# A two-layer hybrid encoder on one core: one head's products with the values a tick later, some priorities moved, and the last output tiles stored in another order

## The chip, the core and the metric

The kernel runs on one core of a Trainium2 chip. Five engines work side by side, each through its own list of instructions in order: TensorE (PE in the profile, with its weight loads as PEld), VectorE (DVE), ScalarE (ACT), GpSimd (POOL) and SyncE (SP), which issues most of the DMAs. An engine waits on a semaphore where it needs another's result. The metric is the device time of one execution, in microseconds (us).

## The reference

Two layers on 512 tokens of width 1024, in float32, then a last norm. Cut to what matters:

```python
for i in range(DEPTH):                                   # 2 layers
    proj = rmsnorm(x, norm_mix[i]) @ w_in[i]
    qa, ka, va, glu_in, qc, kc, vc, gates = split(proj)
    ya = diff_attention(qa, ka, va, ...)                 # 4 heads
    yb = conformer_conv(glu_in, ...)                     # 31 taps, layernorm, silu
    yc = neighbourhood_attention(qc, kc, vc, rpb[i])     # 8 heads, 8 x 16 windows
    ga, gb, gc = split(sigmoid(gates))
    x = x + (ga*(ya @ w_br_a[i]) + gb*(yb @ w_br_b[i]) + gc*(yc @ w_br_c[i])) @ w_o[i]
    h = rmsnorm(x, norm_ffn[i])
    x = x + (silu(h @ w_ffn_gate[i]) * (h @ w_ffn_up[i])) @ w_ffn_down[i]
    x = x + sigmoid(rmsnorm(x, norm_ple[i]) @ w_ple_gate[i]) * (p[i] @ w_ple_in[i])
return rmsnorm(x, norm_final)

def diff_attention(...):   # per head: two score maps of 64 columns each, rotated q and k
    a = softmax(s[:, 0]) - lam * softmax(s[:, 1])
    o = a @ v
    return rmsnorm(o, subln_g) * (1.0 - lam_init)
```

## The kernel before, in words

**Data.** Activations lie transposed: blocks of 128 channels x 512 tokens. Every product runs as three matmuls on a high and a low part (`mm3`, lines 177 to 179): high x high, high x low, low x high. So each operand is split first: ScalarE copies the high part (`act`, line 143), VectorE subtracts it to get the low part (`tt`, line 157). Weights come 128x1024 at a time through three rotating buffers each for the raw, high and low form (names ending in `wr`, `wh`, `wl`), and their loads and splits are issued with a priority far ahead of their use.

**Names.** The first part of a name is the stage: `glu`, `natten` (neighbourhood attention), `diff` (differential attention), `gatea`/`gateb`/`gatec`, `conv`, `mergea`, `wo`, `ffn`, `ple` (the gated input embedding), `pin` (its products). The second part is the buffer: `mm` (3 PSUM buffers), `sc` (2), `tr` (2, for transposes) and `av` (1) are PSUM; `qk`, `x`, `rp`, `e`, `a`, `pt`, `v`, `y`, `t`, `sm`, `rc`, `z` are SBUF.

**What sets the order.** TensorE executes in the order in which the program is written. The other engines' lists are ordered by a scheduler, from priorities that follow the order of writing, unless a `high_priority(offset=...)` moves some ahead. Attention and norms are written as generators (`later`, `run`): after every 4 products of three matmuls (`chunk`), that is 12 matmuls, the program makes one `tick`, and generators whose time has come issue their next piece between the products of the stage that runs then. `yield 2` means: go on two ticks later. The 31 taps of the convolution (`conv_z`, line 160, VectorE) are given out a few at a time behind other VectorE or ScalarE work (`background(after, n)`), and those left over run at the start of `conv`.

**Differential attention.** `diff_in(head)` computes q and k, rotates them (`diff_rp`: four small DMAs per tile exchange 32-row groups, then products with the tables `diff_r` and a sum) and queues four `diff_unit`s, one for each 128 queries. A unit makes two score maps (`diff_sc`, line 808), their maxima (`diff_s`, line 905), the exponentials (`diff_a`, `diff_e`) and their weighted difference; every second unit transposes its half of the weights (`diff_tr`, line 862), splits them (`diff_pt`) and multiplies them with the values (`diff_av`, from `diff_pt` and `diff_v`). After the second half follows the head's norm (`norm`): the squares `diff_ss` are transposed (line 213), summed (`diff_sm`, line 215), scaled, raised to a power on GpSimd (`diff_rc`, line 222), and spread over all rows by four more transposes (line 226). `diff_v` splits the values for all heads, the last tile of tokens last.

**The end.** The last two blocks of `ple` and the last norm run on tiles of 128 tokens (`final`): for each tile `finish` computes the gate and the norm's column, and `store` scales the row's three parts and writes them: the low half (512 columns, ScalarE and its DMA queue), the middle and high quarters (VectorE, written from SP).

Of the kernel before, what the change touches and what calls it, by code (L numbers as in the profile page):

```python
# [14 lines left out]
AF = mybir.ActivationFunctionType  # L15
ALU = mybir.AluOpType
# [4 lines left out]
P = 128  # L21
# [4 lines left out]
D = 1024  # L26
KD = 8
# [15 lines left out]
EPS = 1e-6  # L43
# [18 lines left out]
class Net:  # L62
# [143 lines left out]
    def norm(self, sq, n, waits, done, spread=True, eps=None):  # L206


        nc = self.nc
        yield waits[0]  # L210
        st = self.ps("tr", (P, 4, P))
        for c in range(4):
            nc.tensor.transpose(st[:, c, :], sq[:, c * P:(c + 1) * P], self.ident)
        sm = self.sb("sm", [P, 4])
        nc.vector.tensor_reduce(out=sm, in_=st, op=ALU.add, axis=AX.X)
        ms = self.sb("sm", [P, 4])
        if eps is None:
            nc.vector.tensor_scalar(ms, sm, 1.0 / n, EPS, ALU.mult, ALU.add)
        else:
            self.stt(ms, sm, 1.0 / n, eps, ALU.mult, ALU.add)  # L220
        col = self.sb("rc", [P, 4])
        nc.gpsimd.tensor_tensor(col, ms, self.power, ALU.pow)
        yield waits[1]
        bc = self.ps("tr", (P, 4, P))
        for c in range(4):
            nc.tensor.transpose(bc[:, c, :], col[:, c:c + 1].to_broadcast([P, P]), self.ident)
        bc = bc.rearrange("p a b -> p (a b)")
        done(col, self.spread(bc) if spread else bc)
# [394 lines left out]
    def natten_in(self, pr, st, ys):  # L623

        self.phase = "natten"
        st4 = self.sb("qk", [P, 4, 512], F32R)
        k2 = self.sb("x", [P, 2, 512], F32R)
        nats = self.parts_of("kh", [512], 2, F32R)
        for s, off in enumerate((OFF_QC, OFF_KC)):
            ps = self.proj(off + pr * P)  # L630
            f = 1.0 if s else 0.125
            nat, low = nats[s], self.sb("t", [P, 512], F32R)
            if pr == 0:

                t = low.bitcast(F32)
                self.stt(t, ps, f, self.rb, ALU.mult, ALU.mult)
                ps, f = t, 1.0
            self.act(nat, ps, AF.Copy, scale=f)
            self.low = self.stt(low, ps, f, nat.bitcast(F32), ALU.mult, ALU.subtract)
            self.background(self.low, 4 if self.i else 5 * (pr > 0))  # L640
            self.stack(nat, low, st4[:, 2 * s:2 * s + 2], k2 if s else None)
        box = {}
        ys.append(self.sb("y", [P, 2, 512], F32R))
        for n in range(4):
            self.later(self.natten_unit(pr, n // 2, n % 2, st4, k2, st, box, ys[pr]),
                       4 if pr else 6, 2)
# [200 lines left out]
    def diff_unit(self, head, qt, st4, k2, st, box, ys):  # L847

        nc, i = self.nc, self.i
        half, t = qt // 2, qt % 2  # L850
        box[qt] = self.probs(st4, k2, qt, box["s0"])
        if t == 0:
            return
        yield 3
        ats = [box[2 * half], box[2 * half + 1]]
        pps = []
        for kp in range(2):
            pt = self.ps("tr", (P, 2, 256))
            for u in range(2):
                for t in range(2):  # L860
                    kc = 2 * kp + u
                    nc.tensor.transpose(pt[:, u, t * P:(t + 1) * P],
                                        ats[t][:, kc * P:(kc + 1) * P], self.ident)
            pp = self.sb("pt", [P, 2, 2, 256], F32R)
            self.split(pp[:, 0], pp[:, 1], pt)
            pps.append(pp)
        yield 2
        if half == 0:
            box["av"] = self.ps("av")
        av = box["av"]  # L870
        cs = slice((head % 2) * P, (head % 2) * P + P)
        for kp in range(2):
            for u in range(2):
                v = st["v"][2 * kp + u][:, head // 2].rearrange("p (a b) -> p a b", a=2)
                self.mm3(av[:, half * 256:half * 256 + 256], v[:, 0, cs], v[:, 1, cs],
                         pps[kp][:, 0, u], pps[kp][:, 1, u], kp * 2 + u == 0, kp * 2 + u == 3)
        if half == 0:
            return

        eps = self.sb("sm", [P, 4])  # L880
        self.stt(eps, box["s0"], EPS, box["s0"], ALU.mult, ALU.mult)
        o = self.sb("t", [P, 512])
        sq = self.sb("ss", [P, 512])
        self.act(sq, av, AF.Square)
        self.act(o, av, AF.Copy, scale=self.subg[:, i:i + 1])

        def done(col, bc):
            self.tt(o, o, bc, ALU.mult)
            y = self.sb("y", [P, 2, 512], F32R)
            self.split(y[:, 0, :], y[:, 1, :], o)  # L890
            ys.append(y)

        yield from self.norm(sq, P, (1, 2), done, spread=False, eps=eps)
# [363 lines left out]
    def ple(self, h, x, xs, pairs):  # L1257
        self.phase = "ple"
        nc, i = self.nc, self.i
        last = i == L - 1  # L1260
        hn, st = [], []
        for m in range(KD - 2 * last):
            g = self.sb("t", [P, 512])
            if m < KD - 2 * last:
                pi = self.embedded(m)
            if m != 1:
                pg = self.ps("mm")
            if m == 0:
                nxt = self.ps("mm")
                self.pair((pg, nxt), (self.a["w_pg"][i, 0], self.a["w_pg"][i, 1]), h)  # L1270
            elif m == 1:
                pg = nxt
            else:
                self.gemm(pg, self.a["w_pg"][i, m], h)

            def gate(pg=pg, g=g):
                self.tt(g, pg, self.rb, ALU.mult)
                self.act(g, g, AF.Sigmoid, table="sigmoid")

            self.ready(gate)  # L1280
            if last and m == 3:
                self.gains()
            def rest(m=m, pi=pi, g=g):
                self.tt(g, g, pi, ALU.mult)
                self.tt(x[m], x[m], g, ALU.add)
                if last:
                    hn.append(self.sb("h", [P, 512]))
                    self.act(hn[m], x[m], AF.Copy, scale=self.par(0, "fin", m))
                    self.sumsq(m, x[m], st)
                else:  # L1290
                    nc.sync.dma_start(xs[m], x[m])
                    hn.append(self.norm_chunk(m, x[m], self.par(i + 1, "mix", m), FIRST[1][m], st))

            self.ready(rest)
        if last:
            return self.final(h, x[KD - 2:], pairs, hn, st[0])
        self.i = i + 1
        self.main_norm(st[0], (3, 2), x=x)
        return hn
# [10 lines left out]
    def final(self, h, x, pairs, hn, most):  # L1310
# [3 lines left out]
        nc, i, mm = self.nc, self.i, self.nc.tensor.matmul  # L1314
# [14 lines left out]
        rbs = self.col  # L1329
# [16 lines left out]

        def finish(t):
            g = self.sb("t", [P, 256])
            self.act(g, pgs[t], AF.Sigmoid, table="sigmoid", scale=rbs[:, t:t + 1])
            self.tt(g, g, pis[t], ALU.mult)  # L1350
            v = self.sb("a", [P, 256])
            self.tt(v, g, pair[t][:, 256:], ALU.add)
# [3 lines left out]
                out=q, in0=v, in1=v, scale=1.0, scalar=0.0, op0=ALU.mult, op1=ALU.add,  # L1356
                accum_out=s)
            ms = self.sb("sm", [P, 1])
            self.stt(ms, s, 1.0 / D, part[:, t:t + 1], ALU.mult, ALU.add)
            col = self.sb("rc", [P, 1])  # L1360
            nc.gpsimd.tensor_tensor(col, ms, self.power[:, 0:1], ALU.pow)
            vs.append(v)
            columns.append(col)

        def store(t):
            col, two = columns[t], pair[t]
            r, out = rows[t], self.a["out"][t * P:(t + 1) * P]
            self.act(r[:, 0:512], low[t], AF.Copy, scale=col)
            nc.scalar.dma_start(out[:, 0:512], r[:, 0:512])
            self.stt(r[:, 768:], vs[t], col, self.gain, ALU.mult, ALU.mult)  # L1370
            if t == 3:
                nc.sync.dma_start(out[:, 768:], r[:, 768:])
            nc.vector.tensor_scalar(r[:, 512:768], two[:, 0:256], col, None, ALU.mult)
            end = 768 if t == 3 else D
            nc.sync.dma_start(out[:, 512:end], r[:, 512:end])

        pair, low, pgs, vs, columns = [], [], [], [], []
        places = ("av", "mm", "av", "sc")
        def inputs(t):
            pis.append(self.ps("sc", (P, 256)))  # L1380
# [6 lines left out]
        for t in range(4):  # L1387
# [4 lines left out]
            products(pg, wg, h, t, range(4))  # L1392
            if t == 1:
                chunks(0)
            if t in (1, 2):
                low.append(turn(places[t - 1], hn[0:4], t - 1))
            products(pg, wg, h, t, range(4, 8 if t == 3 else 6))
            if t == 1:
                sums = self.ps("mm", (P, 4))
# [15 lines left out]
                finish(0)  # L1415
            if t:
                finish(t)
            if t in (1, 2):
                store(t - 1)
        for t in (2, 3):  # L1420
            low.append(turn(places[t], hn[0:4], t))
            store(t)
        return None


# [112 lines left out]
```

## Time and profile before

| | |
|---|---|
| time, median of 3 runs | 1781.59 us (1780.82 to 1783.68) |
| the profiled execution's own time | 1781.65 us |
| its span in the trace | 1779.9 us |
| TensorE busy | 1767.4 us, 99% of the span |
| VectorE busy | 1372.7 us, 77% |
| ScalarE busy | 897.9 us, 50% |
| GpSimd busy | 63.5 us, 4% |
| instructions | 26531 |
| granted TensorE clock, mean | 1.00 of full speed |
| DMA, mean over the span | 145 GB/s, 257.51 MB |

The page gives busy time by engine, then the chain of work that ended last, followed back from the last instruction. A row of a timeline is: start, duration, engine, line, operation, result and sources (without buffer numbers), how many in a row, and in brackets how long the engine was idle before it and what ended that. Matmuls overlap in the pipe, so the time that one costs is the step from its start to the next start.

### The profile page before, as it was taken

Reading aid. Unit: us, or ns where it says so; the run is one execution under the profiler, and the core shown is the slowest. Engines: PE = TensorE matmul, PEld = TensorE weight load, DVE = VectorE, ACT = ScalarE, POOL = GpSimd, SP = SyncE. Lnnn points to the kernel's source line nnn. Section 1 sums busy time; section 2 is a strip of 40 time slices with the busy share of each in tenths; the row PEclk is TensorE's granted clock in tenths of the full one; section 3 lists DMA queues with packets and bytes.
Section 4 is the critical chain, followed back from the end, with each engine's and each line's share of the span. In section 5 each row is a group of like instructions: output and inputs, shape, how many; then the busy total and the mean of one; then the engine's idle time right before and its main releaser. Section 6 shows DMA issues by size and latency. Waiting matters only on the chain.

```text
span 1779.9 us, 26531 instructions
## 1 busy us (share of the span) xinstructions
PE 1767.4 (99%) x10019; PEld 1551.4 (87%) x10019; DVE 1372.7 (77%) x2113; ACT 897.9 (50%) x1480; POOL 63.5 (4%) x102
## 2 busy tenths in 40 slices
PE   9999999999999999999999999999999999999998
PEld 7888888888899899898878888888888998998987
DVE  7789787897877577577786788879878775775776
ACT  5566555425665255255545664563356652542544
POOL 0000000000010000000000000000000100100000
PEclk9999999999999999999999999999999999999999
DMA  5767443325556366253437564433363662663332
GB/s 190 190 180 189 125 130 93 104 97 163 198 157 180 131 166 189 79 141 115 159 121 189 177 181 119 133 87 107 101 199 133 196 190 84 186 181 107 116 110 95
DMA packets 98384, 257.51 MB, mean 145 GB/s; under 512 B 12880, under 2 KB 17616, under 8 KB 98256
## 3 DMA queue, kind: packets, MB, share of 16 engines
q1 hardware_dynamic: 90912, 231.00, 41.4%
q0 software_dynamic: 6336, 23.07, 7.1%
q8 instruction: 79, 1.29, 0.3%
q10 hardware_dynamic: 1008, 1.75, 0.3%
q14 instruction: 49, 0.40, 0.1%
HBM read 216.44 MB, written 7.86 MB: 126 GB/s over the span
## 4 chain that ended last, share of the span: by engine, by line
PE 96%; DVE 2%; issue 1%; DMA 0%; ACT 0%; SPq 0%; POOL 0%; POOLq 0%; DVEq 0%; ACTq 0%
PE ffn_sc L1100 14%; PE ffn_av L1100 7%; PE ffn_mm L177 4%; PE ffn_mm L178 4%; PE ffn_mm L179 4%; PE ffn_tr L1100 4%; PE mergea_mm L179 2%; PE mergea_mm L177 2%; PE mergea_mm L178 2%; PE wo_mm L178 2%; PE wo_mm L179 2%; PE wo_mm L177 2%; PE gateb_mm L178 2%; PE gateb_mm L179 2%; PE gateb_mm L177 2%; PE natten_mm L177 1%
## 5 line engine op out<-in xcount | busy, mean ns | idle before, releaser
L143 ACT ACTIVATE ffn_wh<-ffn_wr 128x1024 fp32r<-128x1024 f32 (+1 forms) x114 | 117.3, 1029 | 183.2 <-PE ffn_mm L178 102.7
L160 DVE SCALAR_TENSOR_TENSOR conv_z<-glu_z,pre_par,conv_z 128x512 f32<-128x512 f32 x240 | 179.3, 747 | 3.0
L157 DVE TENSOR_TENSOR ffn_wl<-ffn_wr,ffn_wh 128x1024 fp32r<-128x1024 f32 (+1 forms) x114 | 135.0, 1184 | 46.5 <-ACT ffn_wh L143 46.0
L1100 PE MATMUL ffn_sc<-wo_h,ffn_wh 128*128 128x256 f32 x704 | 130.4, 283 | 0.0
L1100 PEld LDWEIGHTS ffn_sc<-wo_h,ffn_wh 128*128 128x128 f32 x704 | 110.4, 192 | 0.8
L1100 PE MATMUL ffn_sc<-wo_h,ffn_wl 128*128 128x256 f32 x352 | 99.6, 283 | 0.0
L177 PE MATMUL ffn_mm<-ffn_z,ffn_wh 128*128 128x512 f32 x240 | 93.4, 389 | 0.0
L178 PE MATMUL ffn_mm<-ffn_z,ffn_wh 128*128 128x512 f32 x240 | 93.4, 389 | 0.0
L179 PE MATMUL ffn_mm<-ffn_z,ffn_wl 128*128 128x512 f32 x240 | 93.4, 389 | 0.0
L157 DVE TENSOR_TENSOR ffn_t<-ffn_mm,wo_r 128x512 f32<-128x512 f32 x48 | 33.1, 689 | 72.3 <-PE ffn_mm L179 72.3
L157 DVE TENSOR_TENSOR ffn_wl<-ffn_rp,ffn_wh 128x1024 fp32r<-128x1024 f32 x44 | 53.8, 1222 | 30.1 <-ACT ffn_wh L143 30.1
L143 ACT ACTIVATE mergea_wh<-mergea_wr 128x1024 fp32r<-128x1024 f32 (+1 forms) x32 | 27.1, 847 | 88.8 <-PE mergea_mm L178 80.4
L1100 PEld LDWEIGHTS ffn_sc<-wo_h,ffn_wl 128*128 128x128 f32 x352 | 67.5, 192 | 0.0
L1100 PE MATMUL ffn_sc<-wo_qk,ffn_wh 128*128 128x256 f32 x352 | 67.1, 283 | 0.0
L1100 PE MATMUL ffn_sc<-wo_v,ffn_wh 128*128 128x256 f32 x352 | 67.1, 283 | 0.0
L1100 PE MATMUL ffn_av<-wo_h,ffn_wh 128*128 128x256 f32 x352 | 65.3, 283 | 0.0
L143 ACT ACTIVATE ffn_wh<-ffn_rp 128x1024 fp32r<-128x1024 f32 x44 | 46.4, 1055 | 29.4 <-PE ffn_mm L178 17.5
L905 DVE TENSOR_REDUCE diff_s<-diff_sc 128x1 f32<-128x512 f32 x64 | 42.7, 685 | 16.1 <-PE diff_sc L808 15.9
L1100 PEld LDWEIGHTS ffn_sc<-wo_qk,ffn_wh 128*128 128x128 f32 x352 | 54.9, 192 | 0.0
L1100 PEld LDWEIGHTS ffn_av<-wo_h,ffn_wh 128*128 128x128 f32 x352 | 54.9, 192 | 0.0
L1100 PEld LDWEIGHTS ffn_sc<-wo_v,ffn_wh 128*128 128x128 f32 x352 | 54.9, 192 | 0.0
L179 PEld LDWEIGHTS ffn_mm<-ffn_z,ffn_wl 128*128 128x128 f32 x240 | 45.1, 188 | 9.4
(726 smaller groups left out, 5635.4 us busy)
## 6 DMA issues: line engine op xcount, KB each, us to landing
ffn_wr<-w_gu SPq DMA_DIRECT2D x66, 512.0 KB, 4.2
ffn_e<-w_gu SPq DMA_DIRECT2D x32, 512.0 KB, 3.4
ffn_e<-w_gu POOLq DMA_DIRECT2D x32, 512.0 KB, 8.0
ffn_wr<-w_fd SPq DMA_DIRECT2D x32, 512.0 KB, 4.7
natten_wr<-w_in SPq DMA_DIRECT2D x16, 512.0 KB, 4.5
natten_b<-bias SPq DMA_DIRECT2D x32, 256.0 KB, 4.3
gatec_wr<-w_in SPq DMA_DIRECT2D x16, 512.0 KB, 4.4
diff_wr<-w_in SPq DMA_DIRECT2D x16, 512.0 KB, 4.7
```

The source lines that it names most:

```text
L143: i = self.nc.scalar.activation(out, in_, func, **kw)
L157: return self.nc.vector.tensor_tensor(out, a, b, op)
L160: return self.nc.vector.scalar_tensor_tensor(out, a, s, b, op0, op1)
L177: mm(out, wh, ah, start=first, stop=False)
L178: mm(out, wh, al, start=False, stop=False)
L179: mm(out, wl, ah, start=False, stop=last)
L905: nc.vector.tensor_reduce(out=m[:, u:u + 1], in_=sc, op=ALU.max, axis=AX.X, negate=True)
L1100: mm(bank[:, u], w[:, u, kp], t, start=begin and n == 0, stop=False, skip_group_check=True)
```

## The change

There are five edits:

- **A.** In `diff_unit`, head 0's first half waits 3 ticks in place of 2 ahead of its products with the values. The 12 matmuls `diff_av` change places with 12 matmuls `diff_mm`, in both layers.
- **B.** For the last block of `ple` in the first layer, the gate and what follows it are issued with a priority 14 ahead.
- **C.** In `norm`, the scaling of the row sums is issued with a priority 30 ahead.
- **D.** In the second layer, the first two of the four `natten_in` calls give out 3 taps instead of 4 behind each of their two splits; the four taps taken away are left to `conv`.
- **E.** At the end, tile 1's transposes move from the middle of tile 2's products to behind all products, and its low half is written then. Tile 2's middle quarter is scaled on ScalarE in place of VectorE, and tile 2's scalings are held behind tile 3's gate and norm column.

```diff
         sm = self.sb("sm", [P, 4])
         nc.vector.tensor_reduce(out=sm, in_=st, op=ALU.add, axis=AX.X)
         ms = self.sb("sm", [P, 4])
-        if eps is None:
-            nc.vector.tensor_scalar(ms, sm, 1.0 / n, EPS, ALU.mult, ALU.add)
-        else:
-            self.stt(ms, sm, 1.0 / n, eps, ALU.mult, ALU.add)
+        with self.tc.high_priority(offset=30):
+            if eps is None:
+                nc.vector.tensor_scalar(ms, sm, 1.0 / n, EPS, ALU.mult, ALU.add)
+            else:
+                self.stt(ms, sm, 1.0 / n, eps, ALU.mult, ALU.add)
         col = self.sb("rc", [P, 4])
         nc.gpsimd.tensor_tensor(col, ms, self.power, ALU.pow)
         yield waits[1]
...
                 ps, f = t, 1.0
             self.act(nat, ps, AF.Copy, scale=f)
             self.low = self.stt(low, ps, f, nat.bitcast(F32), ALU.mult, ALU.subtract)
-            self.background(self.low, 4 if self.i else 5 * (pr > 0))
+            self.background(self.low, 3 + (pr > 1) if self.i else 5 * (pr > 0))
             self.stack(nat, low, st4[:, 2 * s:2 * s + 2], k2 if s else None)
         box = {}
         ys.append(self.sb("y", [P, 2, 512], F32R))
...
             pp = self.sb("pt", [P, 2, 2, 256], F32R)
             self.split(pp[:, 0], pp[:, 1], pt)
             pps.append(pp)
-        yield 2
+        yield 2 + (head == half == 0)
         if half == 0:
             box["av"] = self.ps("av")
         av = box["av"]
...
                 self.tt(g, pg, self.rb, ALU.mult)
                 self.act(g, g, AF.Sigmoid, table="sigmoid")
 
-            self.ready(gate)
+            ahead = 14 * (m == KD - 1)
+            with self.tc.high_priority(offset=ahead):
+                self.ready(gate)
             if last and m == 3:
                 self.gains()
             def rest(m=m, pi=pi, g=g):
...
                     nc.sync.dma_start(xs[m], x[m])
                     hn.append(self.norm_chunk(m, x[m], self.par(i + 1, "mix", m), FIRST[1][m], st))
 
-            self.ready(rest)
+            with self.tc.high_priority(offset=ahead):
+                self.ready(rest)
         if last:
             return self.final(h, x[KD - 2:], pairs, hn, st[0])
         self.i = i + 1
...
 
         def finish(t):
             g = self.sb("t", [P, 256])
-            self.act(g, pgs[t], AF.Sigmoid, table="sigmoid", scale=rbs[:, t:t + 1])
+            gated = self.act(g, pgs[t], AF.Sigmoid, table="sigmoid", scale=rbs[:, t:t + 1])
             self.tt(g, g, pis[t], ALU.mult)
             v = self.sb("a", [P, 256])
             self.tt(v, g, pair[t][:, 256:], ALU.add)
...
                 out=q, in0=v, in1=v, scale=1.0, scalar=0.0, op0=ALU.mult, op1=ALU.add,
                 accum_out=s)
             ms = self.sb("sm", [P, 1])
-            self.stt(ms, s, 1.0 / D, part[:, t:t + 1], ALU.mult, ALU.add)
+            ends.append((gated, self.stt(ms, s, 1.0 / D, part[:, t:t + 1], ALU.mult, ALU.add)))
             col = self.sb("rc", [P, 1])
             nc.gpsimd.tensor_tensor(col, ms, self.power[:, 0:1], ALU.pow)
             vs.append(v)
             columns.append(col)
 
-        def store(t):
+        def store_low(t):
+            r, out = rows[t], self.a["out"][t * P:(t + 1) * P]
+            self.act(r[:, 0:512], low[t], AF.Copy, scale=columns[t])
+            nc.scalar.dma_start(out[:, 0:512], r[:, 0:512])
+
+        def store_high(t):
             col, two = columns[t], pair[t]
             r, out = rows[t], self.a["out"][t * P:(t + 1) * P]
-            self.act(r[:, 0:512], low[t], AF.Copy, scale=col)
-            nc.scalar.dma_start(out[:, 0:512], r[:, 0:512])
-            self.stt(r[:, 768:], vs[t], col, self.gain, ALU.mult, ALU.mult)
+            high = self.stt(r[:, 768:], vs[t], col, self.gain, ALU.mult, ALU.mult)
             if t == 3:
                 nc.sync.dma_start(out[:, 768:], r[:, 768:])
-            nc.vector.tensor_scalar(r[:, 512:768], two[:, 0:256], col, None, ALU.mult)
+            if t == 2:
+                self.behind(self.act(r[:, 512:768], two[:, 0:256], AF.Copy, scale=col), ends[3][0])
+                self.behind(high, ends[3][1])
+            else:
+                nc.vector.tensor_scalar(r[:, 512:768], two[:, 0:256], col, None, ALU.mult)
             end = 768 if t == 3 else D
             nc.sync.dma_start(out[:, 512:end], r[:, 512:end])
 
-        pair, low, pgs, vs, columns = [], [], [], [], []
+        pair, low, pgs, vs, columns, ends = [], [], [], [], [], []
         places = ("av", "mm", "av", "sc")
         def inputs(t):
             pis.append(self.ps("sc", (P, 256)))
...
             products(pg, wg, h, t, range(4))
             if t == 1:
                 chunks(0)
-            if t in (1, 2):
-                low.append(turn(places[t - 1], hn[0:4], t - 1))
+            if t == 1:
+                low.append(turn(places[0], hn[0:4], 0))
             products(pg, wg, h, t, range(4, 8 if t == 3 else 6))
             if t == 1:
                 sums = self.ps("mm", (P, 4))
...
                 finish(0)
             if t:
                 finish(t)
+            if t == 1:
+                store_low(0)
             if t in (1, 2):
-                store(t - 1)
-        for t in (2, 3):
+                store_high(t - 1)
+        for t in (1, 2):
             low.append(turn(places[t], hn[0:4], t))
-            store(t)
+            store_low(t)
+        store_high(2)
+        low.append(turn(places[3], hn[0:4], 3))
+        store_low(3)
+        store_high(3)
         return None
 
 
```

Where the scheduler sets the order, the edits show in it at the following places.

VectorE, first layer, from the products of k's rotation for head 2 (`diff_rp_2393`) to the split of its softmax weights. `diff_sm_2468` is the row sum of head 0's norm, `diff_pt_2519` the low part of head 2's first transposed weights, `gatec_wl` the low part of a gate's weights, `conv_z` a tap. Before:

```order
L160 SCALAR_TENSOR_TENSOR conv_z_1492<-glu_z_318,pre_par_67,conv_z_1492 128x512
L157 TENSOR_TENSOR diff_wl_2652<-diff_wr_2650,diff_wh_2651 128x1024
L157 TENSOR_TENSOR diff_rp_2393<-diff_rp_2393,diff_r_1507 128x512
L215 TENSOR_REDUCE diff_sm_2468<-diff_tr_2463 128x4
L157 TENSOR_TENSOR diff_rp_2393<-diff_rp_2393 128x512
L160 SCALAR_TENSOR_TENSOR diff_sm_2470<-diff_sm_2468,diff_sm_2445 128x4
L905 TENSOR_REDUCE diff_s_2474<-diff_sc_2475 128x1
L157 TENSOR_TENSOR diff_rp_2393<-diff_rp_2393,diff_kh_2253 128x512
L905 TENSOR_REDUCE diff_s_2474<-diff_sc_2481 128x1
L160 SCALAR_TENSOR_TENSOR conv_z_1492<-glu_z_318,pre_par_67,conv_z_1492 128x512
L157 TENSOR_TENSOR diff_pt_2519<-diff_tr_2514,diff_pt_2519 128x512
```

In the changed program, the same engine from the last maxima of that stretch:

```order
L157 TENSOR_TENSOR diff_rp_2393<-diff_rp_2393,diff_r_1505 128x512
L160 SCALAR_TENSOR_TENSOR conv_z_1492<-glu_z_318,pre_par_67,conv_z_1492 128x512
L157 TENSOR_TENSOR diff_rp_2393<-diff_rp_2393,diff_r_1507 128x512
L911 RECIPROCAL diff_s_2474<-diff_s_2474 128x1
L160 SCALAR_TENSOR_TENSOR conv_z_1492<-glu_z_318,pre_par_67,conv_z_1492 128x512
L157 TENSOR_TENSOR diff_rp_2393<-diff_rp_2393 128x512
L160 SCALAR_TENSOR_TENSOR diff_s_2474<-diff_s_2474,natten_nlam_540,diff_sm_2000 128x1
L160 SCALAR_TENSOR_TENSOR conv_z_1492<-glu_z_318,pre_par_67,conv_z_1492 128x512
L157 TENSOR_TENSOR diff_rp_2393<-diff_rp_2393,diff_kh_2253 128x512
L160 SCALAR_TENSOR_TENSOR diff_a_2479<-diff_e_2485,diff_s_2474,diff_a_2479 128x512
L157 TENSOR_TENSOR gatec_wl_2736<-gatec_wr_2734,gatec_wh_2735 128x1024
L157 TENSOR_TENSOR diff_pt_2519<-diff_tr_2514,diff_pt_2519 128x512
```

`diff_pt_2519` moved from a place behind one tap and two maxima to one behind the four `diff_rp` steps, three taps, `diff_a` and `gatec_wl`; in the rows ahead of these, `diff_wl_2652` moved from ahead of the row sum `diff_sm_2468` to behind it. The second layer has the same difference.

VectorE, second layer, neighbourhood attention: `natten_pt` and `natten_a` are low parts of transposed softmax weights, `natten_wl` that of weights. Before:

```order
L160 SCALAR_TENSOR_TENSOR conv_z_8801<-glu_z_8700,pre_par_67,conv_z_8801 128x512
L157 TENSOR_TENSOR natten_pt_9385<-natten_tr_9377,natten_pt_9385 128x512
L157 TENSOR_TENSOR natten_wl_9549<-natten_wr_9547,natten_wh_9548 128x1024
L160 SCALAR_TENSOR_TENSOR conv_z_8801<-glu_z_8700,pre_par_67,conv_z_8801 128x512
L157 TENSOR_TENSOR natten_a_9379<-natten_tr_9378,natten_a_9379 64x128
L157 TENSOR_TENSOR natten_y_8992<-natten_av_9422,natten_y_8992 64x256
```

In the changed program:

```order
L160 SCALAR_TENSOR_TENSOR conv_z_8801<-glu_z_8700,pre_par_67,conv_z_8801 128x512
L157 TENSOR_TENSOR natten_pt_9381<-natten_tr_9373,natten_pt_9381 128x512
L157 TENSOR_TENSOR natten_a_9375<-natten_tr_9374,natten_a_9375 64x128
L157 TENSOR_TENSOR natten_wl_9545<-natten_wr_9543,natten_wh_9544 128x1024
L157 TENSOR_TENSOR natten_y_8990<-natten_av_9418,natten_y_8990 64x256
```

`natten_a` moved from behind `natten_wl` and a tap to the place right behind `natten_pt`; one tap is gone from here.

VectorE at the end of the program: `ple_y_16961` is tile 2's output row, `ple_y_16962` tile 3's, `ple_t_17174` (before) and `ple_t_17167` (changed) tile 3's gate. Before:

```order
L160 SCALAR_TENSOR_TENSOR ple_sm_17128<-ple_s_17126,ple_sm_17036 128x1
L160 SCALAR_TENSOR_TENSOR ple_y_16961<-ple_a_17123,ple_rc_17130,ple_b_16843 128x256
L1373 TENSOR_SCALAR ple_y_16961<-ple_tr_17102,ple_rc_17130 128x256
L157 TENSOR_TENSOR ple_t_17174<-ple_t_17174,ple_sc_17162 128x256
L157 TENSOR_TENSOR ple_a_17177<-ple_t_17174,ple_tr_17169 128x256
L1355 ISA ple_t_17179,ple_s_17180<-ple_a_17177 128x256
L1355 ISA ple_s_17180 128x1
L160 SCALAR_TENSOR_TENSOR ple_sm_17182<-ple_s_17180,ple_sm_17036 128x1
L160 SCALAR_TENSOR_TENSOR ple_y_16962<-ple_a_17177,ple_rc_17184,ple_b_16843 128x256
L1373 TENSOR_SCALAR ple_y_16962<-ple_tr_17169,ple_rc_17184 128x256
```

In the changed program:

```order
L160 SCALAR_TENSOR_TENSOR ple_sm_17123<-ple_s_17121,ple_sm_17036 128x1
L157 TENSOR_TENSOR ple_t_17167<-ple_t_17167,ple_sc_17155 128x256
L157 TENSOR_TENSOR ple_a_17170<-ple_t_17167,ple_tr_17162 128x256
L1359 ISA ple_t_17172,ple_s_17173<-ple_a_17170 128x256
L1359 ISA ple_s_17173 128x1
L160 SCALAR_TENSOR_TENSOR ple_sm_17175<-ple_s_17173,ple_sm_17036 128x1
L160 SCALAR_TENSOR_TENSOR ple_y_16961<-ple_a_17118,ple_rc_17125,ple_b_16843 128x256
L160 SCALAR_TENSOR_TENSOR ple_y_16962<-ple_a_17170,ple_rc_17177,ple_b_16843 128x256
L1384 TENSOR_SCALAR ple_y_16962<-ple_tr_17162,ple_rc_17177 128x256
```

Tile 2's high quarter moved from ahead of tile 3's gate to behind tile 3's norm column `ple_sm`, and its middle quarter is gone from VectorE.

## The prediction

> **What bounds the kernel now.** I read the page first (busy times and the chain that ended last), then the whole list of TensorE's waits, then the timelines of the engines around each of them. Shares on the page:
>
> ```profile
> PE 1767.4 (99%) x10019; PEld 1551.4 (87%) x10019; DVE 1372.7 (77%) x2113; ACT 897.9 (50%) x1480; POOL 63.5 (4%) x102
> PE 96%; DVE 2%; issue 1%; DMA 0%; ACT 0%; SPq 0%; POOL 0%; POOLq 0%; DVEq 0%; ACTq 0%
> ```
>
> TensorE is busy for 99% of the span and carries 96% of the chain that ended last. The change takes no product away from it, so it can only win what TensorE loses in waiting, and what comes behind its last instruction. The waits of TensorE, all of them (total us, times, longest):
>
> ```profile
> PE diff_av L177 <- DVE diff_v L157: 2.8, 2, 1.4
> PE pre_av L325 <- DVE pre_zeror L382: 1.1, 1, 1.1
> PE ple_tr L213 <- DVE ple_ss L157: 1.0, 1, 1.0
> PE natten_mm L598 <- DVE natten_t L160: 0.8, 1, 0.8
> PE natten_av L741 <- issue: 0.5, 1, 0.5
> PE conv_tr L226 <- POOL conv_rc L222: 0.4, 1, 0.4
> ```
>
> Together 6.6 us, so even a change that removed every wait and made none would be worth under 0.4%. Four of these rows are touched: diff_av (part A), ple_tr (B), conv_tr (C), natten_av (D). Part E is the end of the program. About 0.2%, or 3.6 us, is what a measurement of this kernel can tell from no change.
>
> **A, what goes.** The first products of head 0's weights with the values stand in both layers behind a VectorE subtraction; these rows are layer 1's, TensorE's first and VectorE's last:
>
> ```profile
> 1096.87 0.39 PE L179 MATMUL diff_mm<-ple_h,diff_wl 128*128 128x512 f32 x1
> 1098.65 0.36 PE L177 MATMUL diff_av<-diff_pt,diff_v 128*128 128x256 f32 x1 [1.39 <-DVE diff_v L157]
> 1097.82 0.68 DVE L157 TENSOR_TENSOR diff_v<-diff_av,diff_v 128x512 fp32r<-128x512 f32 x1
> ```
>
> Matmuls of 512 columns follow one another every 0.23 us (below), so diff_av could have started at 1097.10 and started at 1098.65: 1.55 us lost, and as much in layer 0. One tick later means that 12 further diff_mm products, 12 x 0.23 = 2.7 us of work that is there anyway, come first. diff_av is then wanted at 1099.8, and diff_v is done at 1098.5. This wait goes, with 1.3 us to spare, and everything behind it on TensorE is due 1.55 us earlier.
>
> **A, what takes its place.** The order of the changed program shows VectorE rearranged between the row sum of head 0's norm (diff_sm) and the fetch of head 2's softmax weights (diff_pt). The transposes that spread the norm's column (diff_tr from diff_rc) write the PSUM slot that this first diff_pt subtraction reads. Their place now:
>
> ```profile
> 1117.95 0.60 PE L213 MATMUL diff_tr<-pre_ident,diff_ss 128*128 128x128 f32 x4
> ...
> 1125.25 0.39 PE L178 MATMUL gateb_mm<-ple_h,gateb_wh 128*128 128x512 f32 x1
> 1125.48 0.39 PE L179 MATMUL gateb_mm<-ple_h,gateb_wl 128*128 128x512 f32 x1
> 1125.88 0.62 PE L226 MATMUL diff_tr<-pre_ident,diff_rc 128*128 128x128 f32 x4
> ```
>
> They were wanted at 1125.71 and began at 1125.88, 0.17 lost. VectorE, in the same stretch:
>
> ```profile
> 1118.19 0.69 DVE L157 TENSOR_TENSOR diff_rp<-diff_rp,diff_r 128x512 f32<-128x512 f32 x1 [0.39 <-DMA diff_rp<-diff_rp]
> ...
> 1121.20 0.68 DVE L215 TENSOR_REDUCE diff_sm<-diff_tr 128x4 f32<-128x512 f32 x1
> 1121.80 0.68 DVE L157 TENSOR_TENSOR diff_rp<-diff_rp 128x512 f32<-128x512 f32 x1
> 1122.40 0.15 DVE L160 SCALAR_TENSOR_TENSOR diff_sm<-diff_sm,diff_sm 128x4 f32<-128x4 f32 x1
> 1122.47 0.68 DVE L905 TENSOR_REDUCE diff_s<-diff_sc 128x1 f32<-128x512 f32 x1
> ...
> 1123.79 0.69 DVE L905 TENSOR_REDUCE diff_s<-diff_sc 128x1 f32<-128x512 f32 x1
> 1124.39 0.74 DVE L160 SCALAR_TENSOR_TENSOR conv_z<-glu_z,pre_par,conv_z 128x512 f32<-128x512 f32 x1
> 1125.05 0.69 DVE L157 TENSOR_TENSOR diff_pt<-diff_tr,diff_pt 128x512 fp32r<-128x512 f32 x1
> 1125.65 0.16 DVE L910 RECIPROCAL diff_s<-diff_s 128x1 f32<-128x1 f32 x1
> 1125.72 0.74 DVE L160 SCALAR_TENSOR_TENSOR conv_z<-glu_z,pre_par,conv_z 128x512 f32<-128x512 f32 x1
> 1126.37 0.22 DVE L160 SCALAR_TENSOR_TENSOR diff_s<-diff_s,natten_nlam,diff_sm 128x1 f32<-128x1 f32 x1
> 1126.50 0.69 DVE L157 TENSOR_TENSOR diff_pt<-diff_tr,diff_pt 128x512 fp32r<-128x512 f32 x1
> 1127.10 1.22 DVE L157 TENSOR_TENSOR gatec_wl<-gatec_wr,gatec_wh 128x1024 fp32r<-128x1024 f32 x1
> 1128.23 0.75 DVE L160 SCALAR_TENSOR_TENSOR diff_a<-diff_e,diff_s,diff_a 128x512 f32<-128x512 f32 x1
> 1128.90 0.68 DVE L157 TENSOR_TENSOR diff_t<-diff_t,diff_tr 128x512 f32<-128x512 f32 x1
> ```
>
> Now diff_pt stands ahead of gatec_wl. In the changed order it stands behind it, and behind all four diff_rp steps and diff_a. That gives two routes to the start of gatec_wl.
>
> Route 1, VectorE's queue. The transposes at 1117.95 end at 1118.55, and with the gain at 1117.0. From start to start of the rows, the queue from there holds: diff_sm's sum 0.60, diff_wl 1.13 (as gatec_wl), diff_sm's scale 0.07, two diff_s reductions 1.20, four diff_rp steps 2.40, three taps 1.98, the reciprocal 0.07, diff_s 0.13, diff_a 0.67; together 8.25. gatec_wl starts at 1125.25.
>
> Route 2, ScalarE. gatec_wl needs gatec_wh, and that needs the last gateb_mm product from the old weights:
>
> ```profile
> 1125.68 1.06 ACT L143 ACTIVATE gatec_wh<-gatec_wr 128x1024 fp32r<-128x1024 f32 x1 [0.23 <-PE gateb_mm L178]
> ```
>
> It started 0.43 after that matmul (1125.25), which is now due at 1123.70: 1124.13, plus 1.06, so gatec_wl cannot start ahead of 1125.2.
>
> The two routes agree. With 1.13 for gatec_wl, diff_pt starts at 1126.4, and the transposes 0.83 behind that (1125.05 to 1125.88 now), at 1127.2. They are wanted at 1125.71 - 1.55 = 1124.16. **The new stall is about 3.05 us in each layer**, and in its queue TensorE holds head 2's next score products and all gate products behind it. Net per layer: 3.05 - 0.17 - 1.55 = +1.3 to +1.4; I take 1.4, for the small steps between engines. Route 2 alone keeps the stall near 3.0, so the lower bound is +1.3. The upper bound: the diff_rp steps of this stretch need rotated copies by DMA, and the row at 1118.19 shows VectorE waiting 0.39 for one. On SP's queue the weights gatec_wr, and for some of them gateb_wr, now stand ahead of three of these small transfers. If they land 1 us too late, the net is +2.4. I take the lower value, because in the new order the first of these steps is only due at 1117.0 + 0.60 + 1.13 + 0.07 + 1.20 = 1120.0, and the row has the copy there at 1118.2. Both layers: **+2.8** (2.6 to 4.8).
>
> **B and C.** In the changed order no engine's instructions are moved by the priorities of the last ple block, and none of the norms but head 0's has its scale moved. The waits of ple_tr (1.0) and conv_tr (0.4) stay: 0, at most -1.4 if the chip did what the order does not say.
>
> **D.** Layer 1's natten_av wait of 0.5 ends with natten_a on VectorE:
>
> ```profile
> 976.36 0.68 DVE L157 TENSOR_TENSOR natten_pt<-natten_tr,natten_pt 128x512 fp32r<-128x512 f32 x1
> 976.97 1.22 DVE L157 TENSOR_TENSOR natten_wl<-natten_wr,natten_wh 128x1024 fp32r<-128x1024 f32 x1
> ...
> 978.86 0.28 DVE L157 TENSOR_TENSOR natten_a<-natten_tr,natten_a 64x128 fp32r<-64x128 f32 x1
> ```
>
> The new order has natten_a right behind natten_pt, at 977.0 instead of 978.86, so the wait goes: **-0.5** (with the start of the pipe at most -0.6). The four taps taken out here run later, ahead of the convolution's norm; 4 x 0.66 = 2.6 us on an engine that is idle for 23% of the span. If that cover were gone, up to 2.6 would come back; the share of idle time says not.
>
> **E.** At the end tile 3's chain stood behind two scalings of tile 2, and the output writes come last:
>
> ```profile
> 1772.49 0.48 DVE L160 SCALAR_TENSOR_TENSOR ple_y<-ple_a,ple_rc,ple_b 128x256 f32<-128x256 f32 x1 [1.05 <-POOL ple_rc L1361]
> 1773.29 0.41 DVE L157 TENSOR_TENSOR ple_t<-ple_t,ple_sc 128x256 f32<-128x256 f32 x1
> 1776.12 0.33 SPq L1372 DMA_DIRECT2D out<-ple_y  x1
> 1773.00:1775.00 2.00, 0.96 (x9) 0.72 (x7) 1.71 (x6) 0.69 (x1) 0.00 (x0) 1.00 0.34 131
> ...
> 1777.00:1778.00 1.00, 0.00 (x0) 0.00 (x0) 0.00 (x0) 0.00 (x0) 0.00 (x0) 1.00 1.06 395
> 1778.00:1780.00 2.00, 0.00 (x0) 0.00 (x0) 0.00 (x0) 0.00 (x0) 0.00 (x0) 0.61 0.18 61
> ```
>
> (The last three rows are stretches: busy time of each engine, then granted clock, DMA share, GB/s.) Without the 0.80 us from 1772.49 to 1773.29, that chain is 0.8 us earlier, and a little more since tile 1's transposes no longer stand ahead of it: 0.95 at best. But tile 1's low half, 256 KB written long before the end until now, is then written among the last: 1.31 MB instead of the last 0.52 MB of tile 3 (128, 128 and 256 KB). By the last two rows the writes run at 395 GB/s, to about 1778.3 (2 us at 61 GB/s are 0.3 us at 395). Counted back, 0.52 MB began at 1777.0, 0.9 behind the issue at 1776.12. Now 1.31 MB take 3.3 us; the first of them can go when TensorE is at its last transposes (it ends with 0.96 us in the stretch from 1773, so near 1774.0), an estimated 1773.9; plus 0.9 and 3.3 they end at about 1778.1. So **-0.2** with full channels, -0.95 with none; I take **-0.4**, nearer the first, since the channels are full in the row.
>
> **Sum.** 2.8 + 0 - 0.5 - 0.4 = +1.9 us. The profiled execution took 1781.65 us, 1.75 around its span, and stands 0.06 above the median of 1781.59, so I count from the median: **1783.5 us**, +0.1%.
>
> **The rivals.** *A larger stall (slower).* The rotated copies land behind the weights by 1 us, in both layers: 4.8 - 0.9 = +3.9, 1785.5 us. It decides from the point where the first diff_rp copy lands later than 1120.0 on the scale above. For it: the row that waits 0.39 on such a DMA already. Against: 1.8 us between the landing there and the need. Chance 0.30, as the new queue on SP has no row in this trace.
>
> *The clock (slower).* TensorE idles for 3 us only at the end: its work ends near 1774.0, the rows have the clock at 1.00 until 1778 and 0.61 on average from there to 1780. Full clock for 0.22 and half for 0.78 of those 2 us gives 0.61, so it fell near 1778.4, some 4.4 us after the last work. A stall of 3.05 stays under that; one of 4.05, with the late copies, nearly reaches it. As much time at half the clock as it took to fall costs 2.2 us in each layer: 1785.5 + 4.4 = 1789.9 us. Chance 0.07. The Trainium skill ("TensorE: Matmul & The Clock Gate", part 1, The HAM clock gate) has the clock halved after an idle window of about 3.4 us that runs freely, and in its section Why this matters for your kernels warns of gaps over some 3 us; by the first the 3.05 us stall is just safe, by the second each layer would pay. The trace's end agrees with the first.
>
> *No new wait (faster).* If the transposes did not need diff_pt's slot, or diff_pt came early all the same, both waits for diff_v are simply gone: -3.1 - 0.5 - 0.4 = -4.0, 1777.6 us; in one layer only, 1.4 - 1.55 - 0.9 = -1.1, 1780.5 us. For it: the row sums start earlier by 1.55 too. Against: gatec_wl stands ahead of diff_pt, and its own source cannot be ready before TensorE is at the transposes. Chance 0.09 for both layers, 0.05 for one.
>
> **How the numbers follow.** Forecast 0.47, larger stall 0.30, clock 0.07, no new wait 0.09 and 0.05, and 0.02 for what I have not seen, half to each side. The forecast's own span goes from 2.6 - 0.6 - 0.95 = +1.0 to 2.8 - 0.2 = +2.6 (D worth nothing, E little), 1782.6 to 1784.2. The range holds this, the larger stall and the case of one layer, 0.82 together, and leaves out the clock and the faster case; at its upper end it adds 1 us for a copy that is later still in one layer: 1780.5 to 1786.5. Faster by over 0.2%: 0.09 + 0.01 = 0.10; within: 0.47 + 0.05 = 0.52; slower: 0.30 + 0.07 + 0.01 = 0.38.
>
> **What would show it.** The row diff_av from diff_v gone from TensorE's waits; in its place diff_tr (the norm's column, 4 transposes) waiting for DVE diff_pt about 2.9 to 3.1 us, twice; natten_av gone; ple_tr and conv_tr as before; the last writes issued some 0.8 us sooner behind TensorE's last matmul, and bytes moving at 395 GB/s from the first to the last of six writes. I am wrong if diff_tr waits under 2 us, or if a row with DMA diff_rp stands ahead of it.

## The result and the profile after

The changed kernel takes 1786.25 us (median of 8 runs, 1785.38 to 1788.21) against 1781.59 us: a ratio of 1.0027, 95% interval 1.0016 to 1.0038, so 4.7 us slower. Its profiled execution took 1785.52 us with a span of 1783.7. That lies inside the range given, but 2.8 us above the forecast. The stall that was forecast is there, to some 0.1 us; what was not expected is what follows it.

TensorE's waits, after:

```profile
PE diff_tr L227 <- DVE diff_pt L157: 6.0, 2, 3.0
PE pre_av L326 <- DVE pre_zeror L383: 1.1, 1, 1.1
PE ple_tr L213 <- DVE ple_ss L157: 1.0, 1, 1.0
PE natten_mm L599 <- DVE natten_t L160: 0.8, 1, 0.8
PE conv_tr L227 <- POOL conv_rc L223: 0.4, 1, 0.4
PE diff_tr L863 <- DVE diff_sm L215: 0.4, 1, 0.4
PE pre_mm L352 <- ACT glu_v L143: 0.3, 1, 0.3
```

The rows of diff_av (2.8) and natten_av (0.5) are gone; ple_tr and conv_tr stand as before; of the three new rows one is by far the longest: the norm's column waits for diff_pt in both layers. Its place in the second layer, the timelines of VectorE, of ScalarE and of TensorE after:

```profile
1119.13 0.69 DVE L215 TENSOR_REDUCE diff_sm<-diff_tr 128x4 f32<-128x512 f32 x1 [2.30 <-PE diff_tr L213]
...
1126.72 0.74 DVE L160 SCALAR_TENSOR_TENSOR diff_a<-diff_e,diff_s,diff_a 128x512 f32<-128x512 f32 x1
1127.38 1.22 DVE L157 TENSOR_TENSOR gatec_wl<-gatec_wr,gatec_wh 128x1024 fp32r<-128x1024 f32 x1
1128.52 1.28 DVE L157 TENSOR_TENSOR diff_pt<-diff_tr,diff_pt 128x512 fp32r<-128x512 f32 x2
```

```profile
1126.14 1.06 ACT L143 ACTIVATE gatec_wh<-gatec_wr 128x1024 fp32r<-128x1024 f32 x1
```

```profile
1125.72 0.39 PE L178 MATMUL gateb_mm<-ple_h,gateb_wh 128*128 128x512 f32 x1
1125.94 0.39 PE L179 MATMUL gateb_mm<-ple_h,gateb_wl 128*128 128x512 f32 x1
1129.35 0.62 PE L227 MATMUL diff_tr<-pre_ident,diff_rc 128*128 128x128 f32 x4 [3.02 <-DVE diff_pt L157]
```

From the row sum to gatec_wl 8.25 us pass with VectorE never idle, diff_pt follows 1.14 later, and the transposes begin at 1129.35, 0.83 behind that. No DMA stands in this stretch. (These are the weights of head 1's first half; the text ahead of the result calls them head 2's. Nothing hangs on the number.)

TensorE in the first layer, and then stretches of it (busy time of each engine, granted clock, DMA share, GB/s):

```profile
242.42 0.39 PE L179 MATMUL gateb_mm<-glu_h,gateb_wl 128*128 128x512 f32 x1
245.75 0.62 PE L227 MATMUL diff_tr<-pre_ident,diff_rc 128*128 128x128 f32 x4 [2.94 <-DVE diff_pt L157]
...
247.73 0.63 PE L178 MATMUL diff_mm<-glu_h,diff_wh 128*128 128x512 f32 x1
248.16 0.63 PE L179 MATMUL diff_mm<-glu_h,diff_wl 128*128 128x512 f32 x1
...
250.77 0.39 PE L177 MATMUL diff_mm<-glu_h,diff_wh 128*128 128x512 f32 x1
251.00 0.40 PE L178 MATMUL diff_mm<-glu_h,diff_wh 128*128 128x512 f32 x1
```

```profile
246.00:247.00 1.00, 1.00 (x8) 0.86 (x7) 1.00 (x3) 0.00 (x0) 0.00 (x0) 0.96 1.64 219
247.00:248.00 1.00, 1.00 (x4) 0.81 (x3) 1.00 (x3) 0.51 (x1) 0.00 (x0) 0.50 0.44 53
...
249.00:250.00 1.00, 1.00 (x4) 0.80 (x3) 0.99 (x3) 0.54 (x2) 0.00 (x0) 0.50 1.06 385
250.00:251.00 1.00, 1.00 (x5) 0.79 (x4) 0.94 (x2) 0.00 (x0) 0.00 (x0) 0.83 0.67 154
251.00:252.00 1.00, 1.00 (x8) 0.91 (x7) 0.03 (x1) 0.00 (x0) 0.00 (x0) 1.00 0.04 6
```

TensorE comes back at 245.75, and 1.2 us later the granted clock goes to half, for 3.4 us: the products step by 0.43 us instead of 0.23. In the second layer an idle time of 3.02 is followed by a clock of 1.00.

Where the 3.8 us between the two spans come from, by the starts of the same instructions in both traces: A's first wait -1.6, its stall +2.9 net of the 0.17 before, half clock +1.7; D -1.0; A in the second layer -1.6 and +3.0; the end -0.3; the opening -0.4; three small shifts of 0.3 to 0.4 near 1080, 1153 and 1470 us, +1.1. That adds up to +3.8.

The other two parts, after. natten_a stands right behind natten_pt, and no wait of natten_av is left:

```profile
978.26 0.69 DVE L157 TENSOR_TENSOR natten_pt<-natten_tr,natten_pt 128x512 fp32r<-128x512 f32 x1
978.98 0.28 DVE L157 TENSOR_TENSOR natten_a<-natten_tr,natten_a 64x128 fp32r<-64x128 f32 x1
```

The end is one unbroken run of writes at 395 to 399 GB/s, as fast as the last writes of before (stretches):

```profile
1779.00:1780.00 1.00, 0.00 (x0) 0.00 (x0) 0.81 (x2) 0.69 (x1) 0.00 (x0) 1.00 1.05 399
1780.00:1781.00 1.00, 0.00 (x0) 0.00 (x0) 0.00 (x0) 0.00 (x0) 0.00 (x0) 1.00 1.04 395
1781.00:1782.00 1.00, 0.00 (x0) 0.00 (x0) 0.00 (x0) 0.00 (x0) 0.00 (x0) 1.00 1.07 398
1782.00:1783.70 1.70, 0.00 (x0) 0.00 (x0) 0.00 (x0) 0.00 (x0) 0.00 (x0) 0.77 0.13 43
```

### The profile page after: what moved, and what is told of

The parts are those of the page before. It is cut to its first block, busy times and chain, and to the rows that moved or that the text cites. A ratio compares the mean times of both kernels' runs of the same rounds, so it can differ in the third digit from the quotient of the medians.

```text
span 1783.7 us, 26531 instructions
## 1 busy us (share of the span) xinstructions
PE 1768.1 (99%) x10019; PEld 1551.4 (87%) x10019; DVE 1372.3 (77%) x2112; ACT 899.0 (50%) x1481; POOL 63.7 (4%) x102
## 4 chain that ended last, share of the span: by engine, by line
PE 96%; DVE 2%; DMA 1%; issue 1%; ACT 0%; SPq 0%; POOL 0%; POOLq 0%; DVEq 0%; ACTq 0%
PE ffn_sc L1101 14%; PE ffn_av L1101 7%; PE ffn_mm L178 4%; PE ffn_mm L177 4%; PE ffn_mm L179 4%; PE ffn_tr L1101 4%; PE mergea_mm L177 2%; PE mergea_mm L179 2%; PE mergea_mm L178 2%; PE wo_mm L178 2%; PE wo_mm L177 2%; PE wo_mm L179 2%; PE diff_mm L177 2%; PE diff_mm L178 2%; PE diff_mm L179 2%; PE natten_mm L177 1%
## 5 line engine op out<-in xcount | busy, mean ns | idle before, releaser
L177 PEld LDWEIGHTS ffn_mm<-ffn_z,ffn_wh 128*128 128x128 f32 x240 | 45.1, 188 | 9.3
```

Of the source, the lines that this page charges most:

```text
L177: mm(out, wh, ah, start=first, stop=False)
```

## The experiments

**Part A alone**, on the kernel before:

```diff
-        yield 2
+        yield 2 + (head == half == 0)
```

> The kernel before with part A alone. Theory (A's new order makes the stall, and the clock falls behind some of the stalls): both waits of diff_av gone, two waits of diff_tr for diff_pt of 2.9 to 3.1 us, 2 x (3.1 - 0.17 - 1.55) = +2.8 us, and 1.6 us more for each of the two at which the granted clock falls to half: 1784.4 to 1787.6 us, most likely 1787.5, as the changed kernel without what D and E save (some 1.5). Rival (the norm's priority, part C, makes the order): no stall, -3.1, 1778.5 us.

1787.67 us (ratio to before 1.0031, 1.0019 to 1.0044). The two waits of diff_tr are there, 2.94 and 3.02, so the norm's priority (C) has no hand in them. The profiled run, the slowest but one at 1788.43 us, has half clock behind both (stretches of 3 us):

```profile
247.00:250.00 3.00, 3.00 (x11) 2.40 (x10) 3.00 (x6) 1.66 (x4) 0.00 (x0) 0.64 0.76 186
1131.00:1134.00 3.00, 3.00 (x12) 2.46 (x11) 3.00 (x6) 1.47 (x4) 0.00 (x0) 0.65 0.83 156
```

**All but part A**, the changed kernel with that line put back:

> The changed kernel with part A undone. Theory: diff_av's two waits of 1.4 back, no wait of diff_tr, clock 1.00 throughout; D saves 0.7 to 1.0 and E 0.4 to 0.7: 1780 us. Rival (the stall belongs to C or to the scheduler's other moves): the waits of diff_tr stay, 1784 us or more.

1780.52 us (0.9993, 0.9984 to 1.0002). The two waits of diff_av are back (1.4 each), none of diff_tr, and the clock is 1.00 to the end of TensorE's work. Against before its trace gains 1.0 us at D and 0.3 at E; B and C show nothing. So A costs 1786.25 - 1780.52 = 5.7 us, twice what stall less gain come to (2.7).

**The split first**, the changed kernel with diff_pt ahead:

```diff
-            self.split(pp[:, 0], pp[:, 1], pt)
+            with self.tc.high_priority(offset=30 * (head == 1 and half == 0)):
+                self.split(pp[:, 0], pp[:, 1], pt)
```

> The changed kernel with the split of head 1's first weights (diff_pt) issued with a priority 30 ahead, so that VectorE has it ahead of the reciprocal, diff_a and gatec_wl. Theory: neither diff_av nor diff_tr waits, clock 1.00: 2 x -1.6 on top of what D and E save, 1777 us. Rival (another wait takes the place at the same spot, for instance of diff_a's reader or of the transposes for gatec_wl): 1780 us or more.

1778.38 us (0.998, 0.9971 to 0.9989): the fastest of all, and faster than before. Neither diff_av on diff_v nor diff_tr on diff_pt is left among the waits. On VectorE the first diff_pt now starts 3.4 us ahead of gatec_wl (its timeline in the second layer):

```profile
1120.62 0.68 DVE L157 TENSOR_TENSOR diff_pt<-diff_tr,diff_pt 128x512 fp32r<-128x512 f32 x1
...
1124.01 1.22 DVE L157 TENSOR_TENSOR gatec_wl<-gatec_wr,gatec_wh 128x1024 fp32r<-128x1024 f32 x1
```

It is 1.4 us short of the 1777 expected. The profiled run has small waits (0.2 to 0.6) in their place, one of them for diff_x by DMA. That run is one of the slower ones (1779.72, of 1776.5 to 1779.8); no trace shows what the faster ones do without, so where the 1.4 us go stays open.

**A stall of 2 us**, the changed kernel with gatec_wl alone moved behind the first diff_pt:

```diff
+            low = self.split(hi[:, :n], lo[:, :n], raw[:, :n])
+            if self.lead is not None and self.phase == "gatec":
+                self.behind(low, self.lead)      # lead: head 1's first diff_pt
+                self.lead = None
...
```

> The changed kernel with gatec_wl held behind the first diff_pt and all else as it is. Theory: the stall is shorter by gatec_wl's 1.13, about 1.95 us in each layer; +0.25 each, less 1.5 for D and E: 1780.5 us, if a stall of 2 us leaves the clock at 1.00. If the clock falls behind such a stall as well, 1.6 more for each: 1782 to 1784 us.

1782.3 us (1.0001, 0.9992 to 1.001); the waits are 1.8 and 1.9. By stall and gain alone 1780.52 + 0.5 = 1781.0 would follow. The profiled run had the clock at 1.00 and took 1780.67. A second profile of the same kernel:

> The kernel with the stall of 2 us once more, for a second profile: its runs scatter from 1780.1 to 1783.7 us and the profiled one (1780.67) had the clock at 1.00 throughout. Theory (chance by the window): a run near 1782 or above shows half clock for some 3.4 us behind one of the two stalls. Rival (a stall of 2 us never lowers the clock): 1.00 throughout again, whatever the time.

It took 1783.26 us. Behind the first stall (1.81 us) the clock stays, behind the second, hardly longer (1.89), it falls (stretches):

```profile
243.00:248.00 5.00, 3.19 (x17) 2.56 (x16) 5.00 (x9) 2.29 (x4) 0.00 (x0) 1.00 0.71 144
1127.00:1129.00 2.00, 2.00 (x7) 1.52 (x6) 2.00 (x4) 0.85 (x2) 0.00 (x0) 0.50 0.84 144
```

So an idle time of 1.9 us can be enough, and the rival here, that it never is, falls.

**The changed kernel once more:**

> The changed kernel once more, for a second profile. Theory (window without a tie to the program): the same two idle times of 2.9 to 3.0 us, and half clock behind the first, the second or both, in no fixed pattern: 1785.4 us with one fall, 1787 with two. Rival (tied to the place): half clock in the first layer only, as in the first profile.

1786.21 us, with the same idle times of 2.94 and 3.02; this time half clock behind the second alone (stretches):

```profile
246.00:249.00 3.00, 3.00 (x15) 2.49 (x14) 3.00 (x6) 1.66 (x4) 0.00 (x0) 1.00 0.82 216
1128.00:1131.00 3.00, 3.00 (x10) 2.44 (x11) 2.84 (x5) 1.34 (x3) 0.00 (x0) 0.55 0.79 221
```

The first profile had it behind the first alone, part A alone behind both. The fall is not tied to the place.

**Stalls put in on purpose**, the kernel before with this at every 16th group of products of the merge, output and feed-forward stages:

```diff
+            for k in range(ks):                       # 2 to 10
+                g = self.nc.gpsimd.memset(self.dummy, 0.0)
+                if k == 0:
+                    self.after(g, self.newest)        # waits for the last matmul
+            self.hold = g                             # the next matmul waits for it
...
```

> The kernel before with stalls of TensorE put in on purpose: in the merge, output and feed-forward stages every 16th group of three matmuls waits for 2 to 10 small fills on GpSimd that themselves wait for the matmul ahead, so that idle times from about 1 to several us stand at many places of one run, some 11 us of work apart. Theory (the granted clock is decided over a running window of about 3.4 us that has no tie to the program): no idle time under some 1.5 us is followed by half clock, those of 4 us and more nearly all are, those between are by chance, and each fall lasts 3.4 us and costs some 1.6 us. Rival (a fixed threshold at about 3 us): all stalls above it are followed by half clock, none below.

That run took 2095.86 us. Every stall of its profile over 0.7 us behind the opening, with the granted clock in the 10 us behind it:

| idle time, us | stalls | followed by half clock |
|---|---|---|
| 0.8 to 1.6 | 32 | 0 |
| 2.0 | 7 | 0 |
| 2.3 to 2.5 | 9 | 2 |
| 2.7 | 9 | 6 |
| 3.1 | 7 | 6 |
| 3.4 to 3.5 | 9 | 8 |
| 3.7 and over | 16 | 16 |

Each fall lasts 3.4 us, or two or three times that behind the longer stalls. One idle time of 2.3 and the same at another place in TensorE's timeline, and the stretch behind the second:

```profile
760.99 0.50 PE L1123 MATMUL ffn_sc<-wo_h,ffn_wh 128*128 128x256 f32 x2 [2.34 <-POOL pre_dummy L122]
...
1694.73 0.79 PE L198 MATMUL ffn_mm<-ffn_z,ffn_wh 128*128 128x512 f32 x1 [2.33 <-POOL pre_dummy L122]
```

```profile
1695.00:1697.00 2.00, 2.00 (x5) 1.55 (x6) 0.00 (x0) 0.00 (x0) 0.00 (x0) 0.50 0.00 0
```

Behind the first the clock stays at 1.00, behind the second it is 0.50. A fixed threshold at 3 us is refuted on both sides: 8 falls behind 2.3 to 2.7, and one of the 3.1 us stalls without.

The traces also show what sorts these cases, and it is less chance than it looks. The granted clock changes only on a grid of 3.413 us: all 77 changes in this trace lie a whole number of such steps behind the first one, to within 0.003 us, and the grid lies differently against the program in every run. What counts is how much of a stall falls into one step. Of the 122 stalls over 0.7 us between matmuls in all ten profiles (openings left out), the 78 that leave at most 1.85 us of idle time within any one step keep the clock at 1.00; of the 44 that leave 1.88 or more, 43 are followed by half clock, each time from the end of a step on. (The exception has 1.882; and behind the very last matmul of this run 1.96 us were not enough.) The first profile of the changed kernel, in stretches that are such steps, the first stall and then the second:

```profile
243.51:246.92 3.41, 1.17 (x8) 1.07 (x9) 3.41 (x6) 0.65 (x2) 0.00 (x0) 1.00 1.04 202
246.92:250.33 3.41, 3.41 (x10) 2.67 (x9) 3.34 (x8) 2.05 (x5) 0.00 (x0) 0.50 0.80 237
...
1124.15:1127.56 3.41, 2.18 (x10) 1.46 (x8) 3.41 (x8) 2.22 (x4) 0.00 (x0) 1.00 0.08 19
1127.56:1130.97 3.41, 1.62 (x10) 1.44 (x11) 3.41 (x5) 0.12 (x1) 0.00 (x0) 1.00 0.83 197
1130.97:1134.38 3.41, 3.41 (x20) 2.96 (x19) 3.34 (x8) 2.05 (x5) 0.00 (x0) 1.00 0.83 223
```

TensorE is idle for 2.24 us of the first step, and the next one runs at 0.50. The second stall, though longer, is divided into 1.23 and 1.79, and the clock stays. An estimate from these numbers: a stall of 3.0 us that lies anywhere against the grid leaves over 1.88 us in one step in some 77% of cases.

**The stall filled**, the changed kernel with work of no effect in TensorE's idle time:

```diff
...
+        for _ in range(fill):                         # 12, for head 0's norm
+            nc.tensor.matmul(self.full, self.zero_r, self.zero_r[:, None, :].to_broadcast([P, 4, P]),
+                             start=False, stop=True, skip_group_check=True)
         bc = self.ps("tr", (P, 4, P))
...
```

> The changed kernel with TensorE's new stall filled: ahead of the transposes that wait for diff_pt, 12 products of zeros (12 x 0.23 = 2.7 us) are added to the gate's finished sum, which they leave as it is. VectorE's order and the place where the transposes can start stay the same. Theory (the surplus over the stall itself is the clock): idle time of 0.3 to 0.5 us in place of 3.0, granted clock 1.00 throughout, and the time falls by what the clock cost, 1.6 us for each fall, some 2.5 us on the mean of runs: 1783.5 us. Rival (the surplus is something else that follows the stall, such as transfers or PSUM traffic): 1786 us as the changed kernel.

1783.65 us (1.0011, 1.0001 to 1.002). The transposes still have to wait for diff_pt, but only 0.3 us behind the zeros (its row of TensorE's waits), and the clock holds (stretches around both places):

```profile
PE diff_tr L230 <- DVE diff_pt L157: 0.5, 2, 0.3
```

```profile
240.00:250.00 10.00, 9.79 (x47) 7.87 (x46) 9.96 (x19) 4.93 (x10) 0.00 (x0) 1.00 0.51 125
1122.00:1132.00 10.00, 9.71 (x47) 7.80 (x46) 9.96 (x19) 4.82 (x9) 0.00 (x0) 1.00 0.56 145
```

12 matmuls more in each layer, and 2.6 us less. VectorE's order and the stall's end are as they were, so these 2.6 us are the clock's.

## Why the prediction was right, and where not

**A, what goes: right.** Both waits for diff_v are gone, and TensorE runs 1.62 us earlier behind them (1.55 expected).

**A, what takes its place: right.** 3.10 and 3.18 us lost at the transposes, against 3.05. Both routes held: 8.25 us on VectorE, and ScalarE's gatec_wh 0.42 behind its matmul (0.43). Net per layer 1.3 to 1.4, as taken. The rival of late copies did not come: the row sum found VectorE idle (2.30 us), and the stretch has no wait for a DMA.

**B and C: right**, nothing. **D:** -1.0 where -0.5 was forecast: the wait went (0.7 with the start of the pipe), and 0.3 us more came from small delays ahead of it that the list of waits does not show. **E: right**, -0.3 against -0.4, and for the reason given: the last write is issued 0.84 us sooner behind TensorE's last matmul, and some 0.5 of that are paid back in bytes.

**The clock: the failed step.** The prediction had the mechanism as a rival but put the point where it decides at 4.4 us of idle time, read from the single fall at the end of the program, and so took a stall of 3.05 for safe (0.07). It is not: in the profiles of the changed kernel and of part A alone, 4 of 6 such stalls were followed by half clock, and each fall costs half of 3.4 us, 1.7 (2.2 had been taken). Forecast without falls: 1783.5; measured with the stall filled: 1783.65. With 1.5 falls in a run (two stalls at the 77% estimated above), 1.5 x 1.7 = 2.6, one gets 1786.1, against 1786.25 measured. The eight runs' mean granted clocks fit that: 0.997 in five of them, as in the profile with two falls (part A alone), and 0.998 or 0.999 in three, as in the profiles with one. The one fall at the end could not show the threshold: TensorE's work ended at 1773.96, only 1.07 us before the end of a step, so the clock fell a whole idle step later, 4.4 us behind the work, and how little idle time would have done does not show.

The Trainium skill ("TensorE: Matmul & The Clock Gate", part 1, The HAM clock gate) says that the clock is halved after at least one idle window of about 3.4 us, and that this window runs freely. The runs agree with the length (steps of 3.413 us, and as much at half speed) and with the free running; they differ on the idle time: a window need not be idle as a whole, 1.9 us of idle time within one were enough.

That the time moved by 4.7 and not 1.9 us also turned "within 0.2%" into "slower": of the chances, that case had 0.38. And that 1786.25 lies inside the range is luck: the upper part of the range, to 1786.5, was there for the late copies, which did not come, and the rival that did, at its price of 1789.9, stood outside.

## What to carry to other kernels

Where one engine is busy for 99%, a step moved on it is paid in the order of the others: look for which in-order queue now has a large job ahead of the small one that frees a buffer, and price the stall by both routes to that job. A TensorE stall of some 1.9 us or more can have a second price, 1.7 us for each fall of the clock. Whether it is paid depends on how the stall lies against the clock's steps of 3.413 us, which no program here controls; all 16 stalls of 3.7 us and over paid it, none under 1.88 did. It does not stand in the list of waits, but in the granted clock of the microseconds behind it. Removing the stall at its source (the split 30 ahead, 1778.38 us) beats both kernels; where it can't be removed, filling it with products that change nothing holds the clock.

## What the runs showed of the hardware that I had not expected

Equal idle times are followed by a fall or not, from run to run and from layer to layer, as the grid of 3.413 us happens to divide them. That adds to the spread of this kernel's time: the runs with a mean clock of 0.999 took 1785.4 and 1785.5 us, those with 0.997 1786.1 to 1788.2. Behind the stalls of 3.0 us the clock comes back after one step of half speed, in which TensorE was busy all the time. And a fall may begin as late as 1.2 us after TensorE is back at work (245.75 and 246.92), so that a look at the clock during the stall alone shows nothing.
